# Two transformer blocks on one core: rank 150 for the attention strips' VectorE and ScalarE steps, and filling products written ahead of block 2's first head

## The chip, the core and the metric

The program runs on one core of a Trainium2 chip. The time is device microseconds of one execution, median of three runs. In the profile PE is TensorE (matrix products), PEld its weight loads, DVE VectorE, ACT ScalarE, POOL GpSimd, and SP the engine that issues the weights' transfers.

## The reference, cut to what matters

Sequence 512, width 1024, float32. Block 1: norm, one projection, forgetting attention with 8 heads of 64 columns beside a gated mixing branch, an output projection, then a convolutional feed-forward layer. Block 2 has the same frame with two kinds of attention, 8 heads each, and its norms are modulated by a vector.

```python
# block 1, per head and block of 128 queries
logits = q @ k.T * Dh**-0.5 + ci[:, None] - c_k      # c: running sum of log_f; causal mask
o      = softmax(logits) @ v
h = x + concat([att, sg]) @ w_out
h = h + conv_ffn(rmsnorm(h, g), w_up, conv_w, conv_b, w_down)

# block 2
h = modulate(rmsnorm_2(x, g_attn_norm), sh_a, sc_a)
q_lat, kv_lat, k_rope, ca_qkv = split(h @ w_in)
o_mla = mla_attention(q, k, v)          # q, k, v from the latents, normed, rope; chunked causal mask
o_ca  = chunk_attention(cq, ck, cv, rel_bias)
x = x + g_a * (concat([o_mla, o_ca]) @ w_out)
x = x + g_m * ffn(modulate(rmsnorm_2(x, g_mlp_norm), sh_m, sc_m))
```

## The kernel before

**Products.** Each float32 product is three products of rounded halves (high by high, high by low, low by high), all accumulated in PSUM. Weights arrive in pieces of 128 x 1024 by SP's queue (`load_split`, line 338), ScalarE rounds a piece (line 347, tile whi) and VectorE or GpSimd subtracts to get the rest (line 348, tile wlo). `weights` (line 358) always asks for two pieces more than it takes. Four buffers hold split pieces.

**Attention** is cut into strips of 128 queries of one head, four to a head (64 strips in block 2, 32 in block 1), and `attention` (line 612) goes through them a turn at a time. Turn t: prepare heads that are up to `ahead` strips away (line 626: transposes, then the splits of `stack`, lines 665 to 669, or lines 1639 to 1643); scores of strip t (TensorE) with the minimum over keys of bias minus scores on VectorE (line 590, read straight from PSUM) and the exponential on ScalarE (line 594), which needs the minimum; a portion of background work (line 632); half of the turn's filling products (line 633); the transposes of strip t-1's exponentials (line 603) and their copy to SBUF (line 605); the other half of the filling products; the value products of strip t-2. After a pair of heads, `pair_end` divides by the sums (lines 685, 687), transposes (695) and splits the result (711, 712) for the output projection.

**Filling products** (`Fill fill`) are other projections, in block 2: cq1, ck1, mla0, cv1, mla1, then the output projection's parts out0, out1 and out. out1 needs results of the first eight heads. Each step yields its nominal time in ns, and `run(ns)` runs steps until their sum has passed ns. One step of cq1 is six products of 256 columns, counted as 658 ns. **Background work** (`Fill bg`) is norms and rotations on VectorE and GpSimd: squares on GpSimd (lines 1411, 1500), sums on VectorE, a power of -0.5 on GpSimd (line 523), and products with the result on VectorE (lines 1104, 1423, 1514).

**Order.** TensorE runs its instructions as they are written (line 766). Each other engine's order is fixed when the program is built: a planner walks through a modelled time and, whenever an engine is free, gives it the ready instruction of lowest rank. The rank is the place at which the instruction is written, less the offset of `high_priority`. Before the change, block 1's heads are prepared at offset 40 (`AHEAD`), background work inside `attention` at offset -60 (`BEHIND`), and strips at 0. `nc.any` copies (line 605) leave the engine to the planner. On the chip each engine then keeps to its order and waits on semaphores.

**Block 2's first head.** `block2_mix` runs the latents' projection, cq0 and cv0 with background norms beside them (lines 1466 to 1469). Then `attention` prepares head 0 before any filling product is written:

```python
        hd[0] = heads[0](0)
        fill.run(rate(-1))
```

Head 0 (`ca_head`) transposes ca (line 1596), which line 1423 has just normalized, copies the result out (lines 1599, 1601) and splits it (lines 665 to 669), and only then strip 0 can be scored.

Of the kernel before, what the change touches and what calls it, by code (L numbers as in the profile page):

```python
# [10 lines left out]
F32 = mybir.dt.float32  # L11
# [3 lines left out]
AF = mybir.ActivationFunctionType  # L15
ALU = mybir.AluOpType
# [3 lines left out]
P = 128  # L20
# [206 lines left out]

AHEAD = 40

BEHIND = 60  # L230
HALVES = (slice(0, 256), slice(256, 512))


class Kernel:
# [343 lines left out]
    def strip_scores(self, hd, qi):  # L578

        nc = self.nc  # L580
        nk = (qi + 1) * P
        n = max(nk, 256)
        s = self.bank("s")
        qk = hd["qk"]
        for j, (q, k) in enumerate(qk):
            self.mm(s[:, :n], q[:, qi * P:(qi + 1) * P], k[:, :n], j == 0, j == len(qk) - 1)
        st = self.sm.tile([P, 2], F32, tag="st", name="st", bufs=4)
        parts = hd["bias"](qi)
        for j, (cs, b) in enumerate(parts):
            nc.vector.tensor_tensor_reduce(  # L590
                out=s[:, cs], in0=s[:, cs], in1=b, scale=1.0, scalar=3e38 if j == 0 else st[:, j - 1:j],
                op0=ALU.add, op1=ALU.min, accum_out=st[:, j:j + 1])
        p = self.pp.tile([P, 512], F32, tag="p", name="p")
        nc.scalar.activation(out=p[:, :nk], in_=s[:, :nk], func=AF.Exp, bias=st[:, len(parts) - 1:len(parts)],  # L594
                             scale=-1.0, accum_out=hd["sums"](qi))
        return s, p

    def strip_turn(self, hd, qi, sp):
        nk = (qi + 1) * P
        s, p = sp  # L600
        for kb in range(qi + 1):
            c = slice(kb * P, (kb + 1) * P)
            self.nc.tensor.transpose(s[:, c], p[:, c], self.ident)  # L603
        pt = self.pt.tile([P, 512], F32, tag="pt", name="pt")
        self.nc.any.tensor_copy(out=pt[:, :nk], in_=s[:, :nk])
        return pt

    def strip_values(self, hd, qi, pt, o):
# [3 lines left out]
    def attention(self, heads, fill, rate, bg, bgrate, mix, ahead=2, depth=1):  # L612
# [10 lines left out]
        for t in range(n + depth + 3):  # L623
# [4 lines left out]
            if t < n:  # L628
                h, qi = seq[t]
                sc[t] = self.strip_scores(hd[h], qi)  # L630
            with self.tc.high_priority(offset=-BEHIND):
                bg.run(bgrate(t))
# [46 lines left out]
    def pair_end(self, o, mix, sums, at, pool, tag, half=None):  # L679


        nc = self.nc
        qs = range(4) if half is None else range(2 * half, 2 * half + 2)
        c8, c512 = slice(2 * qs[0], 2 * qs[-1] + 2), slice(qs[0] * P, (qs[-1] + 1) * P)
        nc.vector.reciprocal(sums[:, c8], sums[:, c8])
        att = self.att.tile([P, 512], F32, tag="att", name="att")
        nc.vector.tensor_tensor(out=att[:, c512].rearrange("p (g d) -> p g d", d=64),
                                in0=o[:, c512].rearrange("p (g d) -> p g d", d=64),
                                in1=sums[:, c8].unsqueeze(2).to_broadcast([P, 2 * len(qs), 64]),
                                op=ALU.mult)  # L690

        def turn():
            tp = self.bank("s")
            for t in qs:
                nc.tensor.transpose(tp[:, t * P:(t + 1) * P], att[:, t * P:(t + 1) * P], self.ident)  # L695
            if not half:
                t = pool.tile([P, 2, 512], F32R, tag=tag, name="mix")
                mix[at] = t[:, 0], t[:, 1]
            ins = self.split(mix[at], tp, c512)
            if half:  # L700

                self.before = ins
            mix[at, half] = True
        return turn
# [624 lines left out]
    def block2_mix(self, xn, norm_b, final, evac, evac_last, norm_a):  # L1329
        nc, i = self.nc, self.i  # L1330
# [11 lines left out]
                                       in1=self.col("g_ca_k_2"), op0=ALU.mult, op1=ALU.mult)  # L1342
# [3 lines left out]
                                       in1=self.col("g_mla_k_2")[0:64], op0=ALU.mult, op1=ALU.mult)  # L1346
# [113 lines left out]
        bg = Fill()  # L1460
# [120 lines left out]
        def ca_head(h):  # L1581
            def f(at):
                pr, odd = divmod(h, 2)
                if pr >= 2:
                    fill.upto("ck1")
                    bg.upto("w_ck1")
                elif pr == 0:
                    bg.upto("w_cq0")
                sums, sh = self.sums(pairs, at)
                if pr not in qkf:  # L1590
                    out = []
                    for z, nm in ((0, "qf"), (1, "kf")):
                        b = self.bank()
                        for t in range(4):
                            o = z * 512 + pr * P
                            nc.tensor.transpose(b[:, t * P:(t + 1) * P], ca[t][:, o:o + P], self.ident)
                        t = one.tile([P, 512], F32, tag=nm, name=nm)
                        if z == 0:
                            nc.any.tensor_copy(out=t, in_=b)
                        else:  # L1600
                            nc.scalar.activation(out=t, in_=b, func=AF.Copy, scale=gca)
                        out.append(t)
                    qkf[pr] = out
                bs = two.tile([P, 512], F32, tag="bs", name="bs")
                nc.scalar.dma_start(out=bs, in_=i["relb"][h])
                nc.vector.tensor_scalar(out=bs, in0=bs, scalar1=-1.0, scalar2=None, op0=ALU.mult)
                nc.gpsimd.memset(bs[0:64, 448:512], BIG)

                def bias(qi):
                    n = (qi + 1) * P  # L1610
                    return [(slice(0, n), bs[:, 512 - n:512])]

                def v(kb):
                    if pr >= 2:
                        fill.upto("cv1")
                    return vc[:, kb, h * 64:(h + 1) * 64]

                return dict(qk=self.stack(stk, *qkf[pr], odd), bias=bias, sums=sh,
                            v=v,
                            end=(sums, 4 + pr, one, mix_at[pr]))  # L1620
            return f

        def mla_head(h):
            def f(at):
                pr, odd = divmod(h, 2)
                c, hc = divmod(h, 4)
                fill.upto(f"mla{c}")
                bg.upto(f"mk{c}")
                sums, sh = self.sums(pairs, at)
                m = slice(0, QK)  # L1630
                parts = []
                for src, scale in ((mq[c], None), (mk[c], gml[m])):
                    b = self.bank()
                    for t in range(4):
                        nc.tensor.transpose(b[m, t * P:(t + 1) * P], src[t // 2][:, t % 2, hc], self.ident)  # L1635
                    hi = stk.tile([P, 512], F32R, tag="st", name="hi")[m]
                    lo = stk.tile([P, 512], F32R, tag="st", name="lo")[m]
                    if scale is None:
                        nc.scalar.copy(hi, b[m])
                        nc.vector.tensor_tensor(out=lo, in0=b[m], in1=hi.bitcast(F32), op=ALU.subtract)  # L1640
                    else:
                        nc.scalar.activation(out=hi, in_=b[m], func=AF.Copy, scale=scale)
                        nc.vector.scalar_tensor_tensor(out=lo, in0=b[m], scalar=scale,
                                                       in1=hi.bitcast(F32), op0=ALU.mult, op1=ALU.subtract)
                    parts.append((hi, lo))
                (qh, ql), (kh, kl) = parts

                def bias(qi):
                    n = (qi + 1) * P
                    return [(slice(0, n), mlam[:, 512 - n:512])]  # L1650

                return dict(qk=[(qh, kh), (qh, kl), (ql, kh)], bias=bias, sums=sh,
                            v=lambda kb: vm[c][:, kb, hc * 64:(hc + 1) * 64],
                            end=(sums, pr, one, f"ca{pr}"))
            return f

        heads = [ca_head(h) for h in range(8)] + [mla_head(h) for h in range(8)]
        self.attention(
            heads, fill,
            lambda t: 3000 if t < 0 else 2000 if t < 16 else 1600 if t < 34 else 500,  # L1660
            bg, lambda t: 1700 if t < 16 else 600, mix, ahead=4, depth=1)
        fill.drain()
        ctx.close()
# [31 lines left out]
```

## Time and profile before

| | |
|---|---|
| median of three runs | 1244.67 us (1243.74 to 1245.11) |
| the profiled execution's own time | 1242.75 us |
| its span, first to last instruction | 1240.9 us |
| busy in the span: PE, PEld, DVE, ACT, POOL | 1206.9, 1049.5, 792.5, 539.2, 194.2 us |
| mean granted TensorE clock | 0.989 of full |
| block 1's mixing stage, about | 0 to 232 us |
| block 1's feed-forward layer | 232 to 592 us |
| block 2's mixing stage, its attention | 592 to 880 us, 658 to 855 us |
| block 2's feed-forward layer | 880 to 1241 us |

How to read the profile: PE's busy time is modelled and matmuls overlap, so the gaps in PE's row, with what ended them, say more than its share. A granted clock of 1.00 is 2.4 GHz and 0.50 is 1.2 GHz. "Idle before <- releaser" behind an instruction is the time that its engine did nothing, and the instruction whose end let it go on.

### The profile page before, as it was taken

Reading aid. Unit: us, or ns where it says so; the run is one execution under the profiler, and the core shown is the slowest. Engines: PE = TensorE matmul, PEld = TensorE weight load, DVE = VectorE, ACT = ScalarE, POOL = GpSimd, SP = SyncE. Lnnn points to the kernel's source line nnn. Section 1 sums busy time; section 2 is a strip of 40 time slices with the busy share of each in tenths; the row PEclk is TensorE's granted clock in tenths of the full one; section 3 lists DMA queues with packets and bytes.
Section 4 is the critical chain, followed back from the end, with each engine's and each line's share of the span. In section 5 each row is a group of like instructions: output and inputs, shape, how many; then the busy total and the mean of one; then the engine's idle time right before and its main releaser. Section 6 shows DMA issues by size and latency. Waiting matters only on the chain.

```text
span 1240.9 us, 17330 instructions
## 1 busy us (share of the span) xinstructions
PE 1206.9 (97%) x6730; PEld 1049.5 (85%) x6730; DVE 792.5 (64%) x1415; ACT 539.2 (43%) x963; POOL 194.2 (16%) x208
## 2 busy tenths in 40 slices
PE   9999999999999999999998998899999999999998
PEld 6887878988888888888998897789988888888887
DVE  6555877688888886433666779766676566553221
ACT  6444544444444443223435555664554444442110
POOL 1457400300000000000344452501200000000000
PEclk9999999999999999999999999999999999999999
DMA  7321212156666656433122111110132222233330
GB/s 242 99 86 48 73 68 69 52 190 200 189 202 195 193 185 193 129 94 114 56 103 64 56 69 61 51 35 18 69 119 87 101 102 92 96 94 103 117 110 17
DMA packets 40033, 131.57 MB, mean 106 GB/s; under 512 B 4608, under 2 KB 5504, under 8 KB 39952
## 3 DMA queue, kind: packets, MB, share of 16 engines
q1 hardware_dynamic: 31536, 102.64, 25.2%
q10 hardware_dynamic: 8208, 27.27, 7.1%
q8 instruction: 52, 0.85, 0.3%
q0 software_dynamic: 208, 0.57, 0.2%
q14 instruction: 29, 0.24, 0.1%
HBM read 128.37 MB, written 2.10 MB: 105 GB/s over the span
## 4 chain that ended last, share of the span: by engine, by line
PE 85%; DVE 7%; POOL 4%; ACT 2%; issue 2%; DMA 1%; SPq 0%; POOLq 0%; ACTq 0%; DVEq 0%
PE mm L369 74%; PE s L369 4%; PE o L369 3%; PE s L603 2%; DVE wlo L348 1%; DVE nt L550 1%; DMA x<-in_xT_dram 1%; DVE ca L1423 1%; DVE s L590 0%; POOL ss L523 0%; POOL nw L523 0%; PE s L695 0%; DVE kl L669 0%; DMA cs<-in_c_dram 0%; PE mm L1635 0%
## 5 line engine op out<-in xcount | busy, mean ns | idle before, releaser
L348 DVE TENSOR_TENSOR wlo<-wraw,whi 128x1024 fp32r<-128x1024 f32 (+4 forms) x182 | 210.4, 1158 | 182.0 <-ACT whi L347 181.2
L347 ACT CAST whi<-wraw 128x1024 fp32r<-128x1024 f32 (+4 forms) x194 | 192.2, 994 | 281.3 <-PE mm L369 261.8
L369 PE MATMUL mm<-xnh,whi 128*128 128x512 f32 (+1 forms) x832 | 312.4, 375 | 1.1 <-DVE nt L550 0.6
L369 PE MATMUL mm<-xnl,whi 128*128 128x512 f32 (+1 forms) x832 | 311.0, 374 | 0.0
L369 PE MATMUL mm<-xnh,wlo 128*128 128x512 f32 (+1 forms) x832 | 310.7, 373 | 0.0
L369 PEld LDWEIGHTS mm<-xnh,whi 128*128 128x128 f32 x832 | 157.0, 189 | 28.7 <-PE mm L369 0.8
L369 PEld LDWEIGHTS mm<-xnh,wlo 128*128 128x128 f32 x832 | 157.1, 189 | 27.7
L369 PEld LDWEIGHTS mm<-xnl,whi 128*128 128x128 f32 x832 | 157.2, 189 | 27.1
L369 PE MATMUL mm<-gh,whi 128*128 128x512 f32 (+1 forms) x384 | 141.6, 369 | 1.1 <-DVE x L937 0.6
L369 PE MATMUL mm<-gl,whi 128*128 128x512 f32 (+1 forms) x384 | 141.3, 368 | 0.0
L369 PE MATMUL mm<-gh,wlo 128*128 128x512 f32 (+1 forms) x384 | 141.3, 368 | 0.0
L729 DVE SCALAR_TENSOR_TENSOR cv<-mm,cols,cv 128x510 f32<-128x510 f32 (+1 forms) x176 | 130.4, 746 | 2.6 <-ACT cv L727 0.6
L369 PE MATMUL mm<-whi,xnh 128*128 128x256 f32 (+3 forms) x304 | 97.7, 321 | 0.2 <-ACT xnh L812 0.2
L369 PE MATMUL mm<-wlo,xnh 128*128 128x256 f32 (+3 forms) x304 | 94.3, 310 | 0.2 <-DVE wlo L348 0.2
L369 PE MATMUL mm<-whi,xnl 128*128 128x256 f32 (+3 forms) x304 | 94.2, 310 | 0.1
L369 PEld LDWEIGHTS mm<-gh,whi 128*128 128x128 f32 x384 | 72.4, 188 | 13.6 <-DVE x L937 0.8
L369 PEld LDWEIGHTS mm<-gl,whi 128*128 128x128 f32 x384 | 72.4, 188 | 12.1
L369 PEld LDWEIGHTS mm<-gh,wlo 128*128 128x128 f32 x384 | 72.4, 188 | 12.0
L594 ACT ACTIVATE p<-s,st 128x128 f32<-128x128 f32 (+1 forms) x96 | 50.7, 528 | 69.7 <-DVE st L590 66.7
L998 DVE CUSTOM_DVE_ANT_0 wada<-wada,cs,cols 128x1024 f32<-128x1024 f32 x48 | 61.5, 1282 | 26.9 <-DMA wada<-in_w_ada_dram 26.7
L369 PE MATMUL mm<-mix,whi 128*128 128x256 f32 (+1 forms) x288 | 74.4, 346 | 2.7 <-ACT vm L1563 1.2
L727 ACT ACTIVATE cv<-mm,cols 128x512 f32<-128x512 f32 x88 | 67.6, 772 | 0.2 <-PE mm L369 0.2
(293 smaller groups left out, 1839.1 us busy)
## 6 DMA issues: line engine op xcount, KB each, us to landing
wraw<-in_w_up_dram SPq DMA_DIRECT2D x88, 512.0 KB, 3.4
wada<-in_w_ada_dram ACTq DMA_DIRECT2D x48, 512.0 KB, 3.6
wraw<-in_w_down_dram SPq DMA_DIRECT2D x32, 512.0 KB, 3.5
wraw<-in_w_out_dram SPq DMA_DIRECT2D x16, 512.0 KB, 3.4
wraw<-in_w_down_dram SPq DMA_DIRECT2D x16, 384.0 KB, 3.1
wraw<-in_w_qk_dram SPq DMA_DIRECT2D x8, 512.0 KB, 3.7
wraw<-in_w_v_dram SPq DMA_DIRECT2D x8, 256.0 KB, 4.9
x<-in_xT_dram SPq DMA_DIRECT2D x8, 256.0 KB, 6.4
```

The lines of the kernel that those rows point to most:

```text
L347: nc.scalar.copy(hi[:, :n], raw[:, :n])
L348: (nc.gpsimd if pool else nc.vector).tensor_tensor(out=lo[:, :n], in0=raw[:, :n], in1=hi[:, :n].bitcast(F32), op=ALU.subtract)
L369: self.nc.tensor.matmul(out, lhsT, rhs, start=start, stop=stop, **kw)
L550: self.applied = nc.vector.scalar_tensor_tensor(out=t, in0=x[k][:, cs], scalar=gain(k), in1=r, op0=ALU.mult, op1=ALU.mult).ins
L594: nc.scalar.activation(out=p[:, :nk], in_=s[:, :nk], func=AF.Exp, bias=st[:, len(parts) - 1:len(parts)], scale=-1.0, accum_out=hd["sums"](qi))
L603: self.nc.tensor.transpose(s[:, c], p[:, c], self.ident)
L727: nc.scalar.activation(out=t, in_=ps, func=AF.Identity, scale=w[2], bias=self.col(cb, n))
L729: nc.vector.scalar_tensor_tensor(out=t[:, d:], in0=ps[:, :512 - d], scalar=w[2 - d], in1=t[:, d:], op0=ALU.mult, op1=ALU.add)
L998: nc.vector.tensor_tensor_reduce(out=w, in0=w, in1=self.cs, scale=1.0, scalar=self.col("b_ada_2", n), op0=ALU.mult, op1=ALU.add, accum_out ...
L1423: nc.vector.tensor_tensor(out=v3, in0=v3, op=ALU.mult, in1=ss[:, j, z, t].unsqueeze(2).to_broadcast([P, 4, 64]))
```

## The change

Three places get `high_priority(offset=150)`: a strip's minimum and exponential, the copy of its transposed exponentials, and the division at the end of a pair of heads, in both blocks. In block 2, three rounds of 1200 ns of filling products and 800 ns of background work are written before `attention`, and the first portion inside it is 1500 ns where it was 3000.

```diff
+FIRST = 150
@@ strip_scores
-        for j, (cs, b) in enumerate(parts):
-            nc.vector.tensor_tensor_reduce(
...
-        p = self.pp.tile([P, 512], F32, tag="p", name="p")
-        nc.scalar.activation(out=p[:, :nk], in_=s[:, :nk], func=AF.Exp, bias=st[:, len(parts) - 1:len(parts)],
-                             scale=-1.0, accum_out=hd["sums"](qi))
+        with self.tc.high_priority(offset=FIRST):
+            for j, (cs, b) in enumerate(parts):
+                nc.vector.tensor_tensor_reduce(
...
+            p = self.pp.tile([P, 512], F32, tag="p", name="p")
+            nc.scalar.activation(out=p[:, :nk], in_=s[:, :nk], func=AF.Exp,
+                                 bias=st[:, len(parts) - 1:len(parts)], scale=-1.0,
+                                 accum_out=hd["sums"](qi))
@@ strip_turn
-        self.nc.any.tensor_copy(out=pt[:, :nk], in_=s[:, :nk])
+        with self.tc.high_priority(offset=FIRST):
+            self.nc.any.tensor_copy(out=pt[:, :nk], in_=s[:, :nk])
@@ pair_end
-        nc.vector.reciprocal(sums[:, c8], sums[:, c8])
         att = self.att.tile([P, 512], F32, tag="att", name="att")
-        nc.vector.tensor_tensor(out=att[:, c512].rearrange("p (g d) -> p g d", d=64),
...
+        with self.tc.high_priority(offset=FIRST):
+            nc.vector.reciprocal(sums[:, c8], sums[:, c8])
+            nc.vector.tensor_tensor(out=att[:, c512].rearrange("p (g d) -> p g d", d=64),
...
@@ block2_mix
+        for _ in range(3):
+            fill.run(1200)
+            bg.run(800)
         self.attention(
             heads, fill,
-            lambda t: 3000 if t < 0 else 2000 if t < 16 else 1600 if t < 34 else 500,
+            lambda t: 1500 if t < 0 else 2000 if t < 16 else 1600 if t < 34 else 500,
             bg, lambda t: 1700 if t < 16 else 600, mix, ahead=4, depth=1)
```

## Rows read from the trace of the kernel before

**Rows 1.** The page's first part: busy us, share of the span, instructions.
```profile
PE 1206.9 (97%) x6730; PEld 1049.5 (85%) x6730; DVE 792.5 (64%) x1415; ACT 539.2 (43%) x963; POOL 194.2 (16%) x208
```
**Rows 2.** Stretches of block 2's attention: busy us of each engine (instructions).
```profile
665.00:725.00 60.00, 55.73 (x440) 54.47 (x439) 42.79 (x100) 31.95 (x75) 25.61 (x29) 0.97 0.19 60
725.00:790.00 65.00, 56.72 (x377) 51.30 (x378) 56.94 (x128) 38.20 (x94) 25.76 (x30) 0.95 0.20 70
774.00:789.00 15.00, 11.64 (x87) 10.05 (x86) 11.94 (x31) 9.64 (x27) 7.79 (x8) 1.00 0.20 72
```
**Rows 3.** PE's waits, whole span: total us, times, longest.
```profile
PE s L603 <- ACT p L594: 14.5, 9, 2.9
PE mm L1596 <- DVE ca L1423: 3.4, 2, 2.2
PE s L695 <- DVE att L687: 2.0, 2, 1.5
```
**Rows 4.** Timeline of PE: five of the nine waits for an exponential.
```profile
115.57 0.33 PE L603 MATMUL s<-ident,p 128*128 128x128 f32 x1 [2.90 <-ACT p L594]
...
725.83 0.44 PE L603 MATMUL s<-ident,p 128*128 128x128 f32 x2 [2.46 <-ACT p L594]
...
749.28 0.33 PE L603 MATMUL s<-ident,p 128*128 128x128 f32 x1 [2.89 <-ACT p L594]
...
780.59 0.55 PE L603 MATMUL s<-ident,p 128*128 128x128 f32 x3 [1.40 <-ACT p L594]
...
835.67 0.55 PE L603 MATMUL s<-ident,p 128*128 128x128 f32 x3 [1.29 <-ACT p L594]
```
**Rows 5.** Timeline around block 2's first head: PE, DVE and POOL.
```profile
656.21 5.80 DVE L1423 TENSOR_TENSOR ca<-ca,ssc 128x256 f32<-128x256 f32 x4 [3.02 <-POOL ssc L523]
...
656.23 2.67 POOL L348 TENSOR_TENSOR wlo<-wraw,whi 128x1024 fp32r<-128x1024 f32 x1
...
661.73 1.66 PE L1596 MATMUL mm<-ident,ca 128*128 128x128 f32 x6 [2.17 <-DVE ca L1423]
...
665.64 0.28 PE L369 MATMUL mm<-whi,xnh 128*128 128x256 f32 x1
...
667.57 0.28 PE L369 MATMUL mm<-whi,xnl 128*128 128x256 f32 x1
667.69 0.28 PE L369 MATMUL s<-kh,qs 128*128 128x256 f32 x1
...
665.37 1.38 DVE L669 TENSOR_TENSOR kl<-kf,kh 64x512 fp32r<-64x512 f32 x2
...
683.08 0.76 DVE L1423 TENSOR_TENSOR ca<-ca,ssc 128x256 f32<-128x256 f32 x2 [2.18 <-POOL ssc L523]
```
**Rows 6.** Stretches after two waits: PE's busy us, granted clock, DMA.
```profile
662.00:664.00 2.00, 1.99 (x10) 0.52 0.23 66
664.00:666.00 2.00, 2.00 (x14) 0.63 0.03 8
750.00:752.00 2.00, 2.00 (x14) 0.70 0.40 123
752.00:754.00 2.00, 1.83 (x9) 0.50 0.35 139
```
**Rows 7.** Timeline before the wait at 749 us: PE's score, DVE's queue.
```profile
742.64 0.28 PE L369 MATMUL s<-kl,qs 128*128 128x256 f32 x1
...
744.48 1.42 DVE L666 TENSOR_TENSOR qs<-qf,qs 64x512 fp32r<-64x512 f32 x1
745.91 2.46 DVE L669 TENSOR_TENSOR kl<-kf,kh 64x512 fp32r<-64x512 f32 x2
748.29 0.28 DVE L590 CUSTOM_DVE_ANT_0 s<-s,bs 128x128 f32<-128x128 f32 x1
```
**Rows 8.** Timeline of DVE before the wait at 725 us.
```profile
723.52 0.96 DVE L1514 TENSOR_TENSOR mqk<-mqk,nw 128x768 f32<-128x768 f32 x1 [3.03 <-POOL nw L523]
724.40 0.56 DVE L590 CUSTOM_DVE_ANT_0 s<-s,bs 128x384 f32<-128x384 f32 x1
```
**Rows 9.** DVE's waits for scores, whole span: total us, times, longest.
```profile
DVE s L590 <- PE s L369: 26.6, 28, 3.9
```

More of the change, by code (lines that the diff above doesn't have):

```diff
@@ L588, in strip_scores @@
         parts = hd["bias"](qi)
-        for j, (cs, b) in enumerate(parts):
-            nc.vector.tensor_tensor_reduce(
-                out=s[:, cs], in0=s[:, cs], in1=b, scale=1.0, scalar=3e38 if j == 0 else st[:, j - 1:j],
-                op0=ALU.add, op1=ALU.min, accum_out=st[:, j:j + 1])
-        p = self.pp.tile([P, 512], F32, tag="p", name="p")
-        nc.scalar.activation(out=p[:, :nk], in_=s[:, :nk], func=AF.Exp, bias=st[:, len(parts) - 1:len(parts)],
-                             scale=-1.0, accum_out=hd["sums"](qi))
+        with self.tc.high_priority(offset=FIRST):
+            for j, (cs, b) in enumerate(parts):
+                nc.vector.tensor_tensor_reduce(
+                    out=s[:, cs], in0=s[:, cs], in1=b, scale=1.0, scalar=3e38 if j == 0 else st[:, j - 1:j],
+                    op0=ALU.add, op1=ALU.min, accum_out=st[:, j:j + 1])
+            p = self.pp.tile([P, 512], F32, tag="p", name="p")
+            nc.scalar.activation(out=p[:, :nk], in_=s[:, :nk], func=AF.Exp,
+                                 bias=st[:, len(parts) - 1:len(parts)], scale=-1.0,
+                                 accum_out=hd["sums"](qi))
         return s, p
@@ L684, in pair_end @@
         c8, c512 = slice(2 * qs[0], 2 * qs[-1] + 2), slice(qs[0] * P, (qs[-1] + 1) * P)
-        nc.vector.reciprocal(sums[:, c8], sums[:, c8])
         att = self.att.tile([P, 512], F32, tag="att", name="att")
-        nc.vector.tensor_tensor(out=att[:, c512].rearrange("p (g d) -> p g d", d=64),
-                                in0=o[:, c512].rearrange("p (g d) -> p g d", d=64),
-                                in1=sums[:, c8].unsqueeze(2).to_broadcast([P, 2 * len(qs), 64]),
-                                op=ALU.mult)
+        with self.tc.high_priority(offset=FIRST):
+            nc.vector.reciprocal(sums[:, c8], sums[:, c8])
+            nc.vector.tensor_tensor(out=att[:, c512].rearrange("p (g d) -> p g d", d=64),
+                                    in0=o[:, c512].rearrange("p (g d) -> p g d", d=64),
+                                    in1=sums[:, c8].unsqueeze(2).to_broadcast([P, 2 * len(qs), 64]),
+                                    op=ALU.mult)
         def turn():
```

## The prediction

> **What bounds the kernel now.** I read the page's shares first, then the waits of TensorE, then the timeline around the largest of them. TensorE is busy 1206.9 of 1240.9 us [rows 1], so all that this change can win is in 34.0 us of gaps and in time at a lowered clock. The gaps that concern it are waits for strips: 14.5 us for exponentials in nine waits, 3.4 for the normalized ca ahead of block 2's first head, 2.0 for divisions [rows 3]. Most lie in block 2's attention, where TensorE misses 4.3 us of 60 and then 8.3 of 65; in the second stretch VectorE itself is busy 56.9 of 65 us [rows 2]. So VectorE's order matters there, but it has little room: the reader should see a queue that is nearly full, not an idle engine with a wrong order.
>
> A wait also costs clock. After the 3.4 us in front of head 0 the granted clock is 0.52 and 0.63 of 2.4 GHz for two stretches of 2 us, after the wait at 749 us it is 0.70 and 0.50 [rows 6]; 0.50 is the 1.2 GHz level. At full clock that is 2 x 0.48 + 2 x 0.37 = 1.7 us and 0.6 + 1.0 = 1.6 us of lost array time.
>
> **Products ahead of head 0.** Now: the first transposes wait until VectorE ends the normalizing products (656.21 + 5.80 = 662.01), the last of the six begin at the lowered clock, and the first score starts at 667.69, with 30 cq1 products (five steps) between [rows 5]. After: a step is 658 ns to `run`, so 3 x 1200 gives six steps and the 1500 inside gives two: 36 products in front of the transposes, 12 behind. At full clock a product takes (667.57 - 665.64) / 17 = 0.1135 us over 18 products [rows 5], so the 36 take 4.09 us and fill the gap, which begins near 658; the transposes still wait for 662.01. The path to the score is head 0's own: copy, split, last subtraction at 665.37 + 1.38 = 666.75 now. With the six transposes taking half of 1.66 us it is about 0.55 us earlier, 666.2, so the score comes 667.69 - 666.2 = 1.5 us earlier, and 18 more products (18 x 0.1135 = 2.0 us) are done by then: 3.5 us. Two things are to be deducted. First, TensorE has only 12 products (1.4 us) for the 3.4 us between the transposes and the score, so a wait of about 2.0 us appears at the score; if it lowers the clock like the present one, 1.7 us go. I take half, 0.85. Second, products are not made but moved. From 774 to 789 us no filling product is left, since out1 waits for the first eight heads, and TensorE is busy 11.64 of 15 us there [rows 2]; 2.0 us of strip work done in that manner takes 2.0 / 0.776 = 2.6 us, so 0.6 is given back. Net 3.5 - 0.85 - 0.6 = **2.0 us** (bounds: -0.2 with 1.7 and the whole 2.0 deducted; 3.5 with nothing). The three rounds of background work add no instruction: all of head 0's norm was already written during cv0, and the rotation tables' 6000 ns, also written there, leave only a debt. The weights' requests that come with the first step are also the same; ck1's two pieces go to GpSimd, where the first ran at 656.23 anyway.
>
> The four normalizing products took 5.80 us beside that GpSimd split, while two of the same shape took 0.76 us at 683.08 [rows 5]; nothing in the change parts them, so I keep 662.01. The Trainium skill (SBUF — State Buffer, Who interferes with whom) says that a VectorE instruction with two SBUF inputs and a GpSimd instruction that reads SBUF exclude each other, and that the later one fully blocks. If the new order did part them, by that rule four would take 1.5 us, ending at 657.7, and the sum of this change would gain some 2 us more from an earlier score; the trace agrees with the rule, 1.45 against 0.38 us for one.
>
> **Rank of minimum, exponential, copy.** Nothing is removed or added; only the planner's choice between instructions that it holds ready changes. Which waits does that reach? At 749 us: the score ended near 742.9, but the minimum ran at 748.29, behind 1.42 + 2.46 us of a later head's subtractions [rows 7]. These are written in line 626, ahead of the minimum in line 630, so they outrank it now, and 150 reverses that. Moving them back costs nothing while the head they belong to is up to four strips away. Worth 2.89 [rows 4] plus 1.6 of clock, 4.5 at most; I take **3.0**, because part of the low stretch is spent in another wait and the saved time is squeezed into a nearly full VectorE. The wait at 835.67 (1.29) and the four small ones (14.5 - 2.90 - 2.46 - 2.89 - 1.40 - 1.29 = 3.56) [rows 3, 4] are of mixed kinds, a split or the result's subtraction before the minimum: 4.85 at most; I take **2.0**.
>
> Not reached directly are the waits behind GpSimd's power. At 725 us VectorE sat 3.03 us on L1514, which waited for L523, with the minimum next in its queue [rows 8]. That product is written in line 632, behind the minimum, and already ranked 60 later. So the minimum had the better rank and still came second: in the planner's time the score was not there yet. Of the same kind are 115.57, 725.83, 780.59 and one wait for a division: 2.90 + 2.46 + 1.40 + 1.5 = 8.3 us, with clock 3 x 1.7 = 5.1 more. A new order draws these anew: bounds 13.4 gained if all go, 2 x (2.90 + 1.7) = 9.2 lost if two more strips fall behind a power. I take **0**, the middle.
>
> **What is pushed back.** 96 minima, exponentials and copies step ahead of PSUM evacuations and weight splits that TensorE also needs. Cover is the two pieces of lookahead and four PSUM banks. If the planner puts a minimum early and the score is late on the chip, all behind it on VectorE waits: today this is 26.6 us in 28 waits, mean 0.95 [rows 9], mostly hidden. Bounds 0 and a fifth more, 5.3; I take **-1.0**. The division's rank matters only where it is late for the result's transposes, and lies within the 2.0 us of [rows 3], counted above.
>
> **Sum.** 2.0 + 3.0 + 2.0 + 0 - 1.0 = 6.0 us off the profiled execution's own 1242.75: 1236.75. The median of the runs is 1.92 above that execution, so I forecast 1236.75 + 1.92 = 1238.7.
>
> **Rivals.**
> *The powers go too.* If the quicker strips also slip in front of most of the 8.3 us, the time is 1238.7 - 8.3 = 1230.4. For it: scores would come earlier in the planner's time as well. Against: the rank played no part in those orders.
> *Given back.* The minima were mostly not ready in the planner's time, the 749 us wait only moves, and the earlier products are missed at 774 us: 2 - 1 = 1 us gained, 1243.7. For it: VectorE at 88% in the worst stretch.
> *Minimum at the head of the queue.* VectorE waits for a score where a weight split or an evacuation could have run, and TensorE then waits for that. Place: 725 to 790 us. Price 0.95 us for each. The gains of 7.0 are eaten when seven or eight such waits reach TensorE; twelve give 1244.67 - 7.0 + 11.4 = 1249. For it: VectorE has 8.1 us free there; against: lookahead hides most of today's 28. The Trainium skill speaks for this one (TensorE: Matmul & The Clock Gate, Architectural detail: the array is 16× 32×32, not 1× 128×128): VectorE and ScalarE are strictly first in, first out. The 3.03 us in front of the minimum agree.
>
> **How the numbers follow.** What a measurement of this kernel can tell from no change is about 0.2%, 2.5 us: 1242.2 and 1247.2 are the limits. Forecast (1235 to 1242): 0.48. Powers go too (1227 to 1235): 0.20. Given back (1242 to 1247): 0.19. Queue's head (above 1247): 0.13. So faster 0.68, same 0.19, slower 0.13. The range leaves out half of the second and most of the last: 1230 to 1247.
>
> **What would show it.** Right: no wait of L1596 for L1423, 36 products before those transposes, a wait of about 2 us at the first score; the minimum of the strip scored at 742 us ahead of L666 and L669, and no wait there; PE's waits for exponentials down from 14.5 to about 10 us; VectorE's and ScalarE's busy time unchanged. Wrong: that sum unchanged with other strips behind L1423, L1514 or L1104; or waits on weight splits (L347, L348) or evacuations that are not there now.

## The result, and the profile after

The changed kernel takes 1252.33 us, median of six runs, against 1244.2 us before, beside it and also of six: ratio 1.0062, interval 1.0041 to 1.0083. It is slower by 0.6%, where 1238.7 was forecast and 1247 was the top of the range.

The profiled execution took 1252.18 us, its span is 1250.5. First the page's shares, then windows of block 2's attention (columns as in [rows 2]), then TensorE's waits.

```profile
PE 1211.1 (97%) x6730; PEld 1052.6 (84%) x6730; DVE 800.9 (64%) x1431; ACT 532.2 (43%) x947; POOL 192.2 (15%) x208
```

```profile
665.00:725.00 60.00, 55.98 (x440) 54.71 (x441) 44.55 (x108) 31.86 (x77) 30.11 (x34) 0.97 0.19 60
725.00:790.00 65.00, 52.51 (x319) 45.80 (x317) 52.60 (x123) 32.04 (x76) 19.75 (x24) 0.89 0.17 61
790.00:855.00 65.00, 63.20 (x446) 58.40 (x447) 45.29 (x113) 38.66 (x104) 7.80 (x7) 0.95 0.10 33
...
765.00:770.00 5.00, 2.21 (x8) 1.92 (x9) 4.20 (x9) 1.02 (x4) 0.00 (x0) 0.70 0.13 52
770.00:775.00 5.00, 5.00 (x19) 4.26 (x19) 2.56 (x6) 1.11 (x4) 0.87 (x1) 0.61 0.00 0
790.00:795.00 5.00, 3.89 (x13) 3.42 (x14) 4.51 (x11) 2.19 (x6) 1.70 (x2) 0.59 0.28 100
795.00:800.00 5.00, 5.00 (x31) 4.56 (x30) 2.69 (x9) 2.88 (x8) 3.44 (x2) 0.72 0.31 112
```

```profile
PE s L606 <- ACT p L596: 17.4, 11, 3.6
PE mm L370 <- ACT vm L1568: 2.8, 1, 2.8
PE mm L370 <- ACT sq L494: 2.5, 1, 2.5
PE mm L370 <- DVE x L917: 2.5, 1, 2.5
...
PE s L370 <- ACT kh L672: 1.1, 1, 1.1
...
PE s L370 <- DVE kl L673: 0.6, 1, 0.6
```

Line numbers are shifted: L606 is L603 of before, L596 is L594, L592 is L590, L917 is L912, L1506 is L1501, L370 is L369. Up to 725 us nothing is lost. From 725 to 790 TensorE does 4.2 us less than before, although less of VectorE is busy (52.6 against 56.9 us, [rows 2]), and its clock is 0.89 where it was 0.95. So the bound is not VectorE's room; something waits. The waits for exponentials rose from 14.5 to 17.4 us [rows 3] instead of falling to 10, and waits on an evacuation (L1568), on the last norm (L917) and, ahead of the feed-forward layer, on a square (L494) stand beside them. Two of the waits for exponentials lead to the cause.

**The first wait for a buffer.** The timeline of all engines around TensorE's wait at 767.79:

```profile
761.63 0.30 DVE L592 CUSTOM_DVE_ANT_0 s<-s,bs 128x128 f32<-128x128 f32 x1 [0.93 <-PE s L370]
761.84 0.14 DVE L592 DVE_READ_ACCUMULATOR2_ANT st<- 128x1 f32 x1
...
762.76 0.99 POOL L1505 TENSOR_TENSOR sqm<-mqk 128x384 f32<-128x384 f32 x1 [4.97 <-PE s L606]
...
764.06 0.69 DVE L670 TENSOR_TENSOR qs<-qf,qs 64x512 fp32r<-64x512 f32 x1
764.76 0.43 DVE L592 CUSTOM_DVE_ANT_0 s<-s,bs 128x256 f32<-128x256 f32 x1
...
765.27 1.39 DVE L673 TENSOR_TENSOR kl<-kf,kh 64x512 fp32r<-64x512 f32 x2
766.69 0.55 DVE L1506 TENSOR_REDUCE nw<-sqm 128x4 f32<-128x384 f32 x1
...
767.28 0.37 ACT L596 ACTIVATE p<-s,st 128x128 f32<-128x128 f32 x1 [3.99 <-DVE nw L1506]
...
767.79 0.48 PE L606 MATMUL s<-ident,p 128*128 128x128 f32 x1 [2.88 <-ACT p L596]
```

The strip's minimum is done at 761.98, in good time. Its exponential starts only at 767.28, when a sum of squares, L1506, has ended. Nothing in the strip needs that sum. What it needs is a tile: the exponential's `p` and the background's `sqm` are both taken from the pool `self.pp`, tag "p", three buffers. GpSimd had written a square into one of them by 763.75; the sum that reads it, written as background and so ranked last, ran on VectorE behind a split, the next strip's minimum and two more splits. The exponential, first in rank, waits for the holder of its buffer, which is last.

**The second.** The rotation's tile `rt` comes from the same three buffers (same view, 23 us later):

```profile
779.62 0.66 PE L606 MATMUL s<-ident,p 128*128 128x128 f32 x4 [1.37 <-ACT p L596]
...
783.06 0.29 DVE L1327 TENSOR_TENSOR rt<-mqk,tabq 128x128 f32<-128x128 f32 x1
...
784.32 0.29 DVE L1329 TENSOR_TENSOR rt<-mqk,tabq 128x128 f32<-128x128 f32 x1
...
787.15 0.28 DVE L1330 TENSOR_TENSOR rt<-mqk,tabq 128x128 f32<-128x128 f32 x1
...
789.97 0.28 DVE L1331 TENSOR_TENSOR mqk<-rt 128x128 f32<-128x128 f32 x1
790.17 0.28 DVE L1332 TENSOR_TENSOR mqk<-rt 128x128 f32<-128x128 f32 x1
...
790.49 0.47 ACT L596 ACTIVATE p<-s,st 128x256 f32<-128x256 f32 x1 [2.31 <-DVE mqk L1332]
...
791.11 0.69 PE L606 MATMUL s<-ident,p 128*128 128x128 f32 x2 [1.70 <-ACT p L596]
```

Six instructions of 0.28 us (L1327 to L1332), 1.7 us of work, hold the buffer from 783.06 to 790.45, 7.4 us, because minima, copies, splits and a division stand in between.

The two waits are 2.88 + 1.70 = 4.6 us, and the four short windows above are those behind them: the granted clock falls short by 0.30, 0.39, 0.41 and 0.28 of 5 us each, 6.9 us together. In the kernel before an exponential waited for L1501 for at most 0.8 us. Not every wait is followed by a low clock: behind the 1.37 us at 779.62 it stays at 1.00.

```profile
780.00:790.00 10.00, 8.94 (x71) 7.78 (x69) 9.05 (x27) 6.08 (x18) 2.73 (x5) 1.00 0.16 54
```

**Where the loss lies.** TensorE's rows at the end of block 2's mixing stage, changed and then before:

```profile
878.59 0.87 PE L370 MATMUL mm<-mix,wsplit 128*128 128x256 f32 x6
881.99 0.35 PE L370 MATMUL mm<-xnh,whi 128*128 128x256 f32 x1 [2.53 <-ACT sq L494]
...
872.38 0.87 PE L369 MATMUL mm<-mix,wsplit 128*128 128x256 f32 x6
873.89 0.36 PE L369 MATMUL mm<-xnh,whi 128*128 128x256 f32 x1 [0.64 <-DVE nt L550]
```

Of the 9.6 us between the two spans, 6.2 are there when the stage's last products start, and 3.4 come behind them, where TensorE waits 2.53 us for the feed-forward layer's first product. That wait is no wait for an exponential, and what brings it stays open.

### The profile page after: what moved, and what is told of

Its sections match the earlier page's. It is cut to its first block, busy times and chain, and to the rows that moved or that the text cites. A ratio compares the mean times of both kernels' runs of the same rounds, so it can differ in the third digit from the quotient of the medians.

```text
span 1250.5 us, 17338 instructions
## 1 busy us (share of the span) xinstructions
PE 1211.1 (97%) x6730; PEld 1052.6 (84%) x6730; DVE 800.9 (64%) x1431; ACT 532.2 (43%) x947; POOL 192.2 (15%) x208
## 4 chain that ended last, share of the span: by engine, by line
PE 83%; DVE 8%; POOL 3%; ACT 3%; issue 2%; DMA 1%; SPq 0%; ACTq 0%; POOLq 0%; DVEq 0%
PE mm L370 73%; PE s L370 4%; PE o L370 3%; PE s L606 2%; DVE wlo L349 1%; DVE kl L673 1%; DVE s L592 1%; ACT p L596 1%; ACT whi L348 1%; DVE nt L551 1%; DMA x<-in_xT_dram 1%; PE mm L1640 1%; POOL nw L524 0%; POOL ss L524 0%; POOL ssc L524 0%
## 5 line engine op out<-in xcount | busy, mean ns | idle before, releaser
L370 PE MATMUL mm<-xnh,whi 128*128 128x512 f32 (+1 forms) x832 | 312.3, 375 | 2.7 <-ACT sq L494 2.5
L370 PE MATMUL mm<-xnh,wlo 128*128 128x512 f32 (+1 forms) x832 | 310.9, 374 | 0.0
L370 PE MATMUL mm<-xnl,whi 128*128 128x512 f32 (+1 forms) x832 | 310.9, 374 | 0.0
L370 PEld LDWEIGHTS mm<-xnh,whi 128*128 128x128 f32 x832 | 157.4, 189 | 30.4 <-ACT sq L494 2.7
L370 PEld LDWEIGHTS mm<-xnh,wlo 128*128 128x128 f32 x832 | 157.4, 189 | 27.7
L370 PEld LDWEIGHTS mm<-xnl,whi 128*128 128x128 f32 x832 | 157.5, 189 | 26.6
L370 PE MATMUL mm<-gh,whi 128*128 128x512 f32 (+1 forms) x384 | 141.6, 369 | 1.1 <-DVE x L942 0.6
L370 PE MATMUL mm<-gl,whi 128*128 128x512 f32 (+1 forms) x384 | 141.3, 368 | 0.0
L370 PE MATMUL mm<-gh,wlo 128*128 128x512 f32 (+1 forms) x384 | 141.3, 368 | 0.0
L370 PE MATMUL mm<-whi,xnh 128*128 128x256 f32 (+3 forms) x304 | 95.9, 316 | 0.8 <-ACT xnh L817 0.8
L370 PE MATMUL mm<-wlo,xnh 128*128 128x256 f32 (+3 forms) x304 | 93.4, 307 | 0.2 <-DVE wlo L349 0.2
L370 PE MATMUL mm<-whi,xnl 128*128 128x256 f32 (+3 forms) x304 | 93.4, 307 | 0.1
L596 ACT ACTIVATE p<-s,st 128x128 f32<-128x128 f32 (+1 forms) x96 | 50.6, 527 | 93.7 <-DVE st L592 67.8
L370 PE MATMUL mm<-mix,whi 128*128 128x256 f32 (+1 forms) x288 | 78.3, 361 | 7.0 <-ACT vm L1568 2.8
L370 PEld LDWEIGHTS mm<-gh,whi 128*128 128x128 f32 x384 | 72.4, 188 | 13.5 <-DVE x L942 0.8
L370 PEld LDWEIGHTS mm<-gh,wlo 128*128 128x128 f32 x384 | 72.4, 188 | 12.1
L370 PEld LDWEIGHTS mm<-gl,whi 128*128 128x128 f32 x384 | 72.4, 188 | 12.1
```

The costliest lines, as they stand in the source:

```text
L370: self.nc.tensor.matmul(out, lhsT, rhs, start=start, stop=stop, **kw)
```

## The experiments

Eighteen kernels, each timed in five rounds beside the kernel before, whose median beside them was 1243.7 to 1245.0 us. A ratio is to that.

**Which part costs it.** e1 has the products ahead alone, e2 the rank alone, e3 and e4 both parts with the rank in one block only:

```diff
+        self.first = FIRST if ahead < 4 else 0     # e3, in attention(); e4: ahead == 4
...
-        with self.tc.high_priority(offset=FIRST):
+        with self.tc.high_priority(offset=self.first):
```

> The kernel before with the products ahead of block 2's first head alone (three rounds of 1200 and 800 ns, first portion 1500), no rank. Theory R (the rank in block 2 costs it all): 1 to 3 us faster than before, so 1241 to 1243. Theory L (the moved products are missed later and redraw the order of block 2): slower, 1248 to 1253. Theory X (neither alone; the loss comes from both together): within 2.5 us of before.

> The kernel before with the rank of 150 alone, in both blocks, and the old order ahead of block 2's first head. Theory R: slower than before by 8 to 12 us, 1252 to 1256. Theory L: 1 to 5 us faster, 1239 to 1243. Theory X: within 2.5 us of before.

> The changed kernel with the rank of 150 in block 1's strips only; block 2's strips are at 0 and the products ahead stay. Block 1's end was 1.1 us earlier in the changed kernel's trace, so theory R: block 2 as in the kernel with the products alone, less about 1 us: 1240 to 1242. Theory L: 1247 to 1252. Theory X: about 1243.

> The changed kernel with the rank of 150 in block 2's strips only, and the products ahead. Theory R: 1252 to 1255, about 1 us above the changed kernel. Theory L: the same as theory R here. Theory X: the same. A time below 1248 would say that the order in which block 1 ends decides what block 2 does.

Measured: e1 1245.35 us (ratio 1.0004, 0.9988 to 1.0020), e2 1250.46 (1.0044, 1.0027 to 1.0061), e3 1246.73 (1.0016, 1.0002 to 1.0030), e4 1251.72 (1.0048, 1.0030 to 1.0066). The rank in block 2 carries the loss, theory R, though e2 lost 5.5 us and not 8. The products ahead, for which R wanted 1 to 3 us, won nothing, and e3 lies 1.4 us above e1 where R wanted 1 below. A wait of 2.52 us stands in e1 where the feed-forward layer begins, at 873.54, against 0.64 before; the last product of the mixing stage had still come 2.2 us earlier (870.14 against 872.38). It is the wait that the changed kernel has at 881.99.

**What the rank makes late.** Two suspects of the trace, each mended by itself, then both. Q: sixteen products of the last norm (L917) read a PSUM bank; VectorE sat 2.53 us on a minimum whose score was not there, with those products behind it, and TensorE then waited 2.45 us for the bank:

```profile
747.27 2.04 DVE L917 SCALAR_TENSOR_TENSOR x<-x,cols,mm 128x256 f32<-128x256 f32 x5
751.85 0.57 DVE L592 CUSTOM_DVE_ANT_0 s<-s,bs 128x384 f32<-128x384 f32 x1 [2.53 <-PE s L370]
...
754.77 1.65 DVE L917 SCALAR_TENSOR_TENSOR x<-x,cols,mm 128x256 f32<-128x256 f32 x4
...
756.57 0.99 PE L370 MATMUL mm<-mix,whi 128*128 128x512 f32 x2 [2.45 <-DVE x L917]
```

S: the shared buffers. e8 mends them in e1, which has no rank.

```diff
+                        with self.tc.high_priority(offset=400):                  # e5, e7
                             nc.vector.scalar_tensor_tensor(out=x[k][:, cs], ...
...
-                sq = self.pp.tile([P, 512], F32, tag="p", name="sqm")[:, :4 * d]   # e6, e7, e8; so too rt and krt
+                sq = self.pp.tile([P, 512], F32, tag="bg", name="sqm", bufs=2)[:, :4 * d]
```

> The changed kernel, with an offset of 400 for the sixteen products of the last norm (L917), so that no minimum comes between them on VectorE. Theory Q (VectorE idles at the head of its queue for a score, 0.50 and 2.53 us, while these products are ready, and TensorE then waits for the bank that they read): the wait of 2.45 us at 756.57 goes, with about 1.5 us of low clock behind it, 1247.5 to 1249.5. Theory S (the loss is the exponential's buffer, held by a background square): unchanged, 1250 to 1253. Theory N (any redrawn order costs as much): 1246 to 1256 without a trend.

> The changed kernel, with two buffers of their own for the background's squares and rotations in block 2, which shared the three buffers of the exponentials. Theory S: the exponential at 767.28, whose minimum had ended at 761.98, no longer waits for the sum of squares L1506; the wait of 2.88 us goes with some 2 us of clock, and others that sit behind a square too, 1245 to 1249. Theory Q: unchanged, 1250 to 1253, the wait behind L917 stays. Theory N: 1246 to 1256 without a trend.

> The changed kernel with both: the last norm's products in front and the background's own buffers. If Q and S are both right the two gains add: 1242 to 1246. Q alone: 1247.5 to 1249.5. S alone: 1245 to 1249. Theory N: 1246 to 1256.

> The products ahead alone (no rank), with the background's own buffers. Theory S: a shared buffer delays exponentials without the rank too (one of them by four VectorE instructions in the order before), so 1 to 3 us less than the 1245.35 of the products alone: 1242 to 1244.5. Theory Q: no change against the products alone, 1245 to 1246. Theory N: 1242 to 1249.

Measured: e5 1252.18 us (1.0053, 1.0034 to 1.0072), e6 1244.66 (1.0000, 0.9984 to 1.0016), e7 1242.66 (0.9981, 0.9968 to 0.9994), e8 1243.60 (0.9991, 0.9977 to 1.0005). Q alone is worth nothing: in e5 the products run in a row, but an exponential waits 4.7 us for the sum of squares and TensorE 3.56. S alone wins back all that was lost. With S mended too, e7 lies 2.0 us below e6, a difference that their intervals do not part from nothing, and it is 0.2% faster than the kernel before. ScalarE's waits for exponentials in e6, those for strips' own minima first: no square, sum or rotation is left among the releasers (`sums` are those of the softmax, and L1423 only scales).

```profile
ACT p L596 <- DVE st L592: 77.4, 48, 7.8
ACT p L596 <- DVE ssc L1423: 3.4, 2, 2.1
ACT p L596 <- DVE uv L1090: 2.0, 1, 2.0
ACT p L596 <- DVE sums L691: 0.3, 1, 0.3
```

**Is it the buffer, or a lucky order?** Own buffers also let the planner draw a new order. e9 gives them to the kernel before, e10 and e11 split the rank, e12 keeps the shared buffers and lets their holders go first:

```diff
-        with self.tc.high_priority(offset=FIRST):
+        with self.tc.high_priority(offset=0):          # e10: copy and division; e11: minimum and exponential
...
+                with self.tc.high_priority(offset=400):    # e12
                     nc.gpsimd.tensor_tensor(out=sq, in0=v, in1=v, op=ALU.mult)
                     nc.vector.tensor_reduce(out=s2[:, t], in_=sq, axis=AX.X, op=ALU.add)
```

> The kernel before, with two buffers of their own for the background's squares and rotations in block 2; no rank, no products ahead. Theory S (the rank made a fault bite that was there before, one exponential behind a square's sum): little to win here, 1242.5 to 1245. If the shared buffer also cost the kernel before, 1240 to 1242.5. If the separation is a gain of its own that has nothing to do with the rank (rival), it saves here the same 7.6 us that it saved in the changed kernel: 1236 to 1239.

> The changed kernel, with the rank of 150 on the minimum and the exponential alone; the copy and the division are at 0. Theory S: it is the minimum that pushes the square's sum back on VectorE, so most of the loss stays, 1248 to 1252. Rival C (the copies and divisions do it): 1244 to 1246.

> The changed kernel, with the rank of 150 on the copy and the division alone; the minimum and the exponential are at 0. Theory S: near the products alone, 1243.5 to 1246.5. Rival C: 1249 to 1253.

> The changed kernel with the shared buffers kept, but an offset of 400 for the background's squares and their sums (L1505, L1506), so that who holds a buffer of the exponentials gives it back first. Theory S: what matters is how long a square holds the buffer, so nearly all is won back as with buffers of its own, 1243.5 to 1247. Rival (own buffers helped by redrawing the order, not by the wait): 1249 to 1254.

Measured: e9 1246.14 us (1.0018, 1.0004 to 1.0032), e10 1247.36 (1.0024, 1.0009 to 1.0039), e11 1247.41 (1.0035, 1.0021 to 1.0049), e12 1254.08 (1.0081, 1.0059 to 1.0102). e9 refutes the rival that separation is a gain in itself: it costs the kernel before 0.2%, a little more than theory S allowed. But e10 and e11 divide the loss evenly, outside both ranges, and e12 missed theory S by 7 us and came out where a merely redrawn order was to put it (1249 to 1254). Its timeline shows part of the reason:

```profile
778.75 5.44 POOL L1327 TENSOR_TENSOR rt<-mqk,tabq 128x128 f32<-128x128 f32 x1 [1.14 <-DVE mqk L1520]
779.18 0.94 DVE L1520 TENSOR_TENSOR mqk<-mqk,nw 128x768 f32<-128x768 f32 x1
780.05 2.35 DVE L349 TENSOR_TENSOR wlo<-wraw,whi 128x1024 fp32r<-128x1024 f32 x2
...
782.32 0.42 DVE L592 CUSTOM_DVE_ANT_0 s<-s,bs 128x256 f32<-128x256 f32 x1
782.66 0.14 DVE L592 DVE_READ_ACCUMULATOR2_ANT st<- 128x1 f32 x1
782.66 1.22 DVE L349 TENSOR_TENSOR wsplit<-wraw,wsplit 128x1024 fp32r<-128x1024 f32 x1
...
784.15 0.45 POOL L1328 TENSOR_TENSOR rt<-mqk,tabq 128x128 f32<-128x128 f32 x1
...
786.41 0.47 ACT L596 ACTIVATE p<-s,st 128x256 f32<-128x256 f32 x1 [9.80 <-POOL mqk L1332]
...
787.03 0.69 PE L606 MATMUL s<-ident,p 128*128 128x128 f32 x2 [9.48 <-ACT p L596]
```

The squares let go early, but now a rotation on GpSimd holds a shared buffer, and its first product takes 5.44 us beside VectorE's work where the next takes 0.45. TensorE stands still for 9.48 us. Not all of that is the buffer: the strip's own minimum is done only at 782.80, behind two products that had waited for a power and two splits, so the buffer holds the exponential back for the last 3.6 us. e11 is alike at 780.62: TensorE waits 6.90 us, but the minimum is done at 778.99 and the exponential starts at 780.00, so the buffer has 1.0 us of it. Theory S, if right, thus concerns all holders and not the squares alone. That was put to the test by separating the buffers in three more kernels: e13 is e2 with own buffers, e15 is e11 with them, and e14 is e12 with the rotations' tiles alone moved out.

> The rank alone, in both blocks, without the products ahead, and with the background's own buffers in block 2. Theory S (the rank is dear because exponentials then wait longer for buffers that background work holds): no exponential waits for a background sum or rotation, and the 1250.5 of the rank alone falls to 1243 to 1246.5. Theory N (a redrawn order is worth plus or minus 3 us whatever the buffers): 1246 to 1253.

> The kernel with the squares first on the shared buffers (1254), with the rotations' tiles alone moved to two buffers of their own. Theory S: the wait of 9.48 us at the transposes of 787 us, whose exponential waited for the rotation L1332, goes with the clock behind it, 1242.5 to 1246. Theory N: 1248 to 1256.

> The rank on the copy and the division alone, with products ahead, and with the background's own buffers. Theory S: the wait of 6.90 us at 780.62, whose exponential waited 7.22 us for the rotation L1332, goes; 1242 to 1245 where the shared buffers gave 1247.4. Theory N: 1245 to 1251.

Measured: e13 1243.84 us (0.9993, 0.9981 to 1.0005), e14 1245.00 (1.0000, 0.9986 to 1.0014), e15 1245.42 (1.0000, 0.9986 to 1.0013, a little above its range and inside that of theory N). Set side by side, each pair differing by the buffers alone; the last three columns are read from the one profiled execution of each kernel:

| | shared | own | difference | held, us | stage, us | first product waits, us |
|---|---|---|---|---|---|---|
| the changed kernel, e6 | 1.0062 | 1.0000 | -0.62% | 11.0 | -4.0 | 2.53, none |
| last norm first: e5, e7 | 1.0053 | 0.9981 | -0.72% | 7.8 | -4.4 | 2.53, none |
| rank alone: e2, e13 | 1.0044 | 0.9993 | -0.51% | 4.6 | -6.0 | 1.73, none |
| rank of copy and division: e11, e15 | 1.0035 | 1.0000 | -0.35% | 1.5 | -7.4 | none, 2.52 |
| squares first: e12, e14 (rotations moved) | 1.0081 | 1.0000 | -0.81% | 3.6 | -4.3 | 2.52, none |
| no rank, products ahead: e1, e8 | 1.0004 | 0.9991 | -0.13% | 0.2 | -0.5 | 2.52, 2.53 |
| no rank: before, e9 | 1 | 1.0018 | +0.18% | 1.0 | +3.8 | 0.64, 0.63 |

With the rank five pairs of five fall, by 0.35 to 0.81%; without it one falls within its interval and one rises just beyond it. *Held* adds up, over block 2's 64 strips of the kernel with shared buffers, how long an exponential still waits although its minimum is done and ScalarE is free. With own buffers it is nothing, in all ten kernels that have them; e4 and e10 hold 10.2 and 5.5 us, and e3, whose rank is in block 1 alone, 2.1. *Stage* is own less shared in the time from block 1's last product with `mix` to block 2's. The last column is the wait ahead of the feed-forward layer's first product, shared and own.

So exponentials are held wherever block 2 has the rank above shared buffers, and nowhere with own buffers. Three things stay open. The size does not follow the held time: e11 holds 1.5 us and its stage differs by 7.4; in each pair the planner also drew a new order, which moves other waits too. The wait ahead of the feed-forward layer, which comes and goes with the order, is part of four of the five differences: of the 5.5 us between the spans of the changed kernel and e6, 3.8 lie behind the mixing stage. And separation also means five buffers in place of three; five shared ones were not run, so sharing and number are not parted. Brought to one clock by the line in the last section, an estimate, e11 and e15 differ by 0.9 us only and the other four by 4.7 to 6.5; but a lower clock is also what waits bring.

**Can the rest be had?** e16 goes on from e7 and puts the products behind GpSimd's power (L1429, L1520) on GpSimd. e17 is e7 without the products ahead, e18 is e7 without the rank in block 1 (edit as in e4).

```diff
-                nc.vector.tensor_tensor(out=v, in0=v, in1=rq.to_broadcast([P, 2, 4, QK]), op=ALU.mult)   # e16; L1429 too
+                nc.gpsimd.tensor_tensor(out=v, in0=v, in1=rq.to_broadcast([P, 2, 4, QK]), op=ALU.mult)
...
-        for _ in range(3):                                  # e17; first portion 3000 again
-            fill.run(1200)
-            bg.run(800)
```

> The best version so far (rank, products ahead, own buffers, the last norm first; 1242.7), with the products behind GpSimd's power in block 2 (L1429, L1520) moved to GpSimd itself, so that VectorE no longer sits on them for 2.4 to 2.6 us with the next minimum behind. If those waits are what is left: the waits of 3.62 us at 708 and 3.15 at 781.5 go with their clock, and the normalized values come no later, 1235 to 1239. Rival (GpSimd's slower products make the heads late instead, four of 256 and two of 768 columns beside VectorE): 1242 to 1247.

> The rank in both blocks, the background's own buffers and the last norm first, without the products ahead of block 2's first head. If the products ahead are worth the 2 us of the prediction: 1243.5 to 1246, against 1242.7 with them. If they are worth nothing (as they were on the kernel before, 1245.35 against 1244.95): 1241 to 1243.5, since the rank alone with own buffers gave 1243.8 and one wait of 0.68 us behind L917 goes.

> The best version so far (rank, products ahead, own buffers, the last norm first; 1242.7) with the rank in block 2's strips only. Block 1's rank took 1.1 us off block 1 in the changed kernel's trace, but 1.4 us were lost with it by the runs (1246.7 against 1245.35): by the trace 1243.5 to 1245, by the runs 1240.5 to 1242.

Measured: e16 1250.04 us (1.0041, 1.0026 to 1.0056), e17 1247.31 (1.0027, 1.0011 to 1.0043), e18 1242.79 (0.9983, 0.9972 to 0.9995). e16 is above both of its ranges: it moved the queue's head instead of freeing it. VectorE now sits on the rotations, the next instructions that need GpSimd, and the minimum at 725.41 comes behind them, with TensorE waiting 5.28 us until 726.59:

```profile
719.28 0.53 DVE L1328 TENSOR_TENSOR rt<-mqk,tabq 128x128 f32<-128x128 f32 x1 [2.79 <-POOL mqk L1520]
...
723.25 0.42 DVE L1507 TENSOR_REDUCE nw<-sqm 128x4 f32<-128x256 f32 x1 [1.45 <-POOL sqm L1506]
...
725.41 0.42 DVE L592 CUSTOM_DVE_ANT_0 s<-s,bs 128x256 f32<-128x256 f32 x1
```

e17 is outside both of its ranges: 4.6 us above e7 without the products ahead, and 3.5 above e13, from which it differs only by the last norm's rank, which was to help. In its profiled execution the wait ahead of the feed-forward layer is back, 2.51 us, which e7 and e13 do not have. Of such size is what a redrawn order does here by itself, and single experiments of this study are read with that. e18 lies between its two ranges and equals e7: block 1's rank is worth nothing that these runs can tell.

## Why the prediction was wrong

The terms stand as changes of the time. Forecast was -6.0 us in all, and +8.1 was measured.

*Products ahead, -2.0.* The steps were right and the end was wrong. The first transposes' wait is gone, the first score starts at 664.51 instead of 667.69 and waits 1.11 + 0.59 = 1.70 us (2.0 forecast). e1 keeps 2.2 us of this to the end of the mixing stage and has lost it by the end: its span is 1242.0 against 1240.9. The prediction looked for the giving back at 774 us; it came at the start of the feed-forward layer, which no term covered. Why TensorE waits 2.52 us there, while VectorE, ScalarE and GpSimd do the same work 2.23 us earlier than before, is left open. Among kernels with own buffers, pairs that differ by these products alone give -0.27% (e9, e8), +0.07% (e13, e6) and -0.46% (e17, e7), so no single worth can be given for them.

*The wait at 749 us, -3.0, and the small ones, -2.0.* The wait at 749 is gone, as forecast. But the same strip has none in e1 and e9 either, which lack the rank, so the runs do not show that it was the rank that removed it. The sum of the waits for exponentials did not fall, since others came. With the buffers separated, the rank alone is 0.07% faster than the kernel before, 0 within its interval, and 0.25% faster than e9, which differs from it by the rank only: some 3 us, just clear of the two intervals, where the rank's terms came to -4.0.

*Powers' waits, 0.* Right in size, though as the middle of wide bounds, which is partly luck: VectorE still sits up to 3.0 us in front of such products, 20.3 us in all (L1428, L1109, L1519) where it was 21.3, and other strips stand behind them.

*What is pushed back, +1.0, bounds 0 to 5.3.* This is the step that failed. It listed as pushed back "PSUM evacuations and weight splits" and as their cover the lookahead and the PSUM banks. It left out the background's sums and rotations, which hold the strips' own three buffers. It could be read in the kernel: `tag="p"` for the exponential and for `sqm`, `rt` and `krt`. It also priced the delay by VectorE's waits for scores [rows 9], whereas the price falls on ScalarE, as an exponential whose minimum is ready, 11.0 us of it in block 2. The waits that it priced did not grow:

```profile
DVE s L592 <- PE s L370: 25.8, 29, 4.2
```

Measured, the rank costs 5.5 us alone (e2, 1250.46 against 1244.95) and 7.0 on top of the products ahead (1252.33 against 1245.35, e1); separation takes 7.7 away (1244.66, e6), the wait ahead of the feed-forward layer included.

*The clock.* Half of 1.7 us was taken in one place and 1.6 us in another. The two waits followed above cost 4.6 us, and the windows behind them fall short by 6.9 us of clock, while the 1.37 us between them cost none: a wait has no fixed price.

*The rivals.* The minimum at the head of the queue had the right sign, place and nearly the right time, 1249, but by luck: it counted on twelve waits for scores. The 2.53 us at 751.85 are that rival to the letter. But it is not the main cause: e5 mends its largest instance and wins nothing until the buffers are apart, and then 2.0 us, which the intervals do not part from nothing. The rule of the Trainium skill that it leaned on, that VectorE is strictly first in, first out (TensorE: Matmul & The Clock Gate, Architectural detail: the array is 16× 32×32, not 1× 128×128), agrees with e16, where the minimum at 725.41 stands behind 2.79 and 1.45 us of idle time.

In e12 GpSimd's L1327 ends at 784.19, 0.3 us after the last of VectorE's instructions on two SBUF tiles beside it (782.66 + 1.22), and so holds the exponential's buffer the longer. The rule weighed in the prediction, that such an instruction and one of GpSimd shut each other out (the Trainium skill, SBUF — State Buffer, Who interferes with whom), agrees with these rows. In e11 three such products took 1.43 us each beside VectorE's splits (774.32 to 778.59), so how long GpSimd is held up differs.

## What to carry to other kernels

Before an instruction is given a higher rank, list every tile that it must obtain, and ask who else draws from the same pool and at what rank: a high rank above a shared buffer can make the low-ranked holder slower and so the high-ranked taker too. Here separating the pool won the loss back; raising one kind of holder alone (e12) won nothing, and raising all of them was not run. The releaser that a profile names is not the whole wait: see first when the waiting instruction's own data were ready. An order drawn by a planner changes everywhere with any edit, here by some 0.3% without a cause that one could use, so a cause is shown by several pairs that differ in it alone, not by one good or bad run.

## What the runs showed of the hardware

The time of one and the same program followed the granted clock: of 24 runs of the kernel before, those beside e1 to e4, the one at mean clock 0.992 took 1240.64 us and the eight at 0.986 took 1244.94 to 1248.05; a straight line through the 24 gives 0.87 us for each 0.001.

A GpSimd product of 128 x 128 took 0.45 us in one place and 5.44 us in another (e12, L1327 and L1328), and the power of 2.90 us took 4.40 in e16.
